# Moving DRAM sums of the output weights out of the attention stage, in a one-core hybrid encoder layer

## The chip, the core and the metric

One core of a Trainium2 chip runs the kernel. The metric is the device time of one execution in microseconds (us). The engines are named as in the profile: PE is TensorE's matmul side and PEld its weight load, DVE is VectorE, ACT is ScalarE, POOL is GpSimd, SP is SyncE, which here only issues DMAs. A name with a q behind it (SPq, ACTq) is the engine's instruction queue.

## What is computed

```python
h = rms_norm(x, norm_w)                                  # x: 512 tokens x 2048, fp32
q, k, v, g_attn, xr, g_lru = split(h @ w_in)             # 1024, 256, 256, 1024, 1024, 1024 columns
attn = softmax(rope(norm(q)) @ rope(norm(k)).T / sqrt(128)) @ v    # 8 heads over 2 kv heads
lru  = scan_forward + scan_backward of a gated recurrence on conv(xr)
mixed = concat[rms_norm(attn) * silu(g_attn), rms_norm(lru) * silu(g_lru)]
out  = x + mixed @ w_out                                 # w_out: 2048 x 2048
```

## The kernel before, in words

Every fp32 product runs as three matmuls on a high and a low part of each operand (`mm3`, lines 151 to 154). The two parts of a weight tile are made on chip from the loaded tile `wr`: ACT casts it to `wh` (line 216) and DVE subtracts, `wl = wr - wh` (line 217). SP loads the tiles (line 205) into a ring of three places, so that a load waits until DVE has finished with the tile three places before.

PE's instructions stand in the order in which the program writes them. The program interleaves a "fill", which is one of the long projections, with a chain of smaller steps: `weave` takes from the fill as many steps as the chain asks for. A fill step is six matmuls of 512 columns. Stages in order of time in the profile: two groups of the LRU input, the key and value projection, the two groups of queries (about 165 to 252 us), the attention woven into three of the four gate groups (about 270 to 432 us), the fourth gate group (to about 475 us), and the output product to the end.

The output product is done by a scheme with seven products in place of eight, on blocks of 256 tokens and of sums of the weights. The sums are made in DRAM, by DMAs alone. A plain copy puts a block of `w_out` into a DRAM buffer (`copy_to`, line 779, issued by SP), and a DMA with accumulation adds a second block to it (`add_to`, line 782, issued by POOL). The buffers are `t1`, `t2`, `t4`, `t30` and `t31`, each with eight blocks of 128 x 512 (256 KB). `t30` and `t31` are finished by `first_sums` (17 steps), which also copies the first terms into `t1` and `t2`. `last_sums` then does 32 steps: 8 adds into `t2`, 8 copies of `t2` to `t4`, 8 adds into `t1` and 8 adds into `t4`. The output product reads `t1` and `t2` first (lines 850 and 854) and `t4` later (line 875). In the profile these buffers are all called `t`; in the order of instructions further down `t_103` is t1, `t_104` is t2, `t_105` is t4, `t_106` and `t_107` are t30 and t31.

`first_sums` steps at every 8th fill step of the second LRU input group and of the key and value projection, and at every 5th fill step of the queries. `last_sums` steps once for each of the 32 softmax steps of the attention.

The attention works on one head and 128 queries at a time, 32 such units. For one unit, PE makes the scores (`weights`, line 594), DVE the negated maximum `mx` (599), ACT the exponential `p` with its sum `sm` (601), DVE the reciprocal (602), POOL the scaling of `p` (603), and DVE a transposition inside 32 x 32 blocks into `u` (604). Two units, half a head, then go through DRAM to be laid out anew: SP writes `u` to `pd` (612) and reads it back as `pt` in four DMAs (619). ACT casts `pt` to `ph`, DVE makes `pl = pt - ph` (both line 623). When both halves of a head are done, PE multiplies with the values (`values`, line 632): the first matmul reads `ph` (L152 in the profile), the second `pl` (L153), and all other PE work stands behind them. DVE also has the split of the gate weights (217), the evacuation `ev` of finished gate groups (390), the gate products (691) and the split of the next head's queries `q` (553).

The order on PE, and on SP within the attention, is the written one. ACT, DVE and POOL are ordered there by a scheduler with priorities. `tc.issue_after(i)` keeps an instruction from being put ahead of instruction `i`; it adds nothing at run time where both are on one engine. `last_scale` holds the latest scaling of `p` on POOL (603).

Of the kernel before, what the change touches and what calls it, by code (L numbers as in the profile page):

```python
# [14 lines left out]
ALU = mybir.AluOpType  # L15
# [3 lines left out]
SEQ = 512  # L19
# [36 lines left out]
C_Q, C_K, C_GA, C_XR, C_GL = 0, 1024, 1536, 2560, 3584  # L56
# [6 lines left out]
def hybrid_kernel(  # L63
# [20 lines left out]
    nc = tc.nc  # L84
# [54 lines left out]
    def pj():  # L139
        return ps.tile([P, SEQ], F32, tag="pj", name=nm("pj"))  # L140
# [4 lines left out]
    def const(shape, name, dt=F32):  # L145
        return cp.tile(list(shape), dt, tag=name, name=name)
# [4 lines left out]
    def mm3(acc, lh, ll, rh, rl, start, stop):  # L151
        nc.tensor.matmul(acc, lh, rh, start=start, stop=False)  # L152
        nc.tensor.matmul(acc, lh, rl, start=False, stop=False)  # L153
        nc.tensor.matmul(acc, ll, rh, start=False, stop=stop)  # L154
# [8 lines left out]
    nhalf = const([P, 48], "nhalf")  # L163
# [56 lines left out]
    def wload(w, r0, c0):  # L220
        with tc.high_priority(AHEAD):
            (raw,) = wraw(w, r0, c0)
            return [wsplit(raw, k) for k in range(2)]
# [32 lines left out]
    def xchunk(c):  # L256
# [6 lines left out]
        xsquare(xc, c)  # L263
        yield

    def rsqrt_mean(dst, src, n, width):

        nc.gpsimd.tensor_scalar(dst, src, 1.0 / n, EPS, op0=ALU.mult, op1=ALU.add)
        nc.gpsimd.tensor_tensor(dst, dst, nhalf[:, :width], op=ALU.pow)

    rstd = const([P, NT], "rstd")
    rbc = const([P, SEQ], "rbc")
# [26 lines left out]
    def proj_feat(c0, acc, first=None, given={}, take=None):  # L299

        acc += [pj() for _ in range(4)]
        for c in range(KT // 2):
            if c == 0 and first:

                for k, (wh, wl) in enumerate(first):
                    for j, (w, x_) in enumerate(((wh, xh), (wl, xh), (wh, xl))):
                        for e in range(4):
                            nc.tensor.matmul(
                                acc[e], w[:, e * P : (e + 1) * P], x_[k],
                                start=k == 0 and j == 0, stop=False,  # L310
                            )
                            if (j, e) in ((1, 1), (2, 3)):
                                yield c, 2 * k + j - 1
                        if (k, j) == (0, 0):
                            yield None
                continue
            if take:
                ws = take()
            else:
                ws = given[c] if c in given else wload(w_in, c * 2 * P, c0)  # L320
            for e in range(4):
                es = slice(e * P, (e + 1) * P)
                for k, (wh, wl) in enumerate(ws):
                    kk = 2 * c + k
                    mm3(acc[e], wh[:, es], wl[:, es], xh[kk], xl[kk], kk == 0, kk == KT - 1)
                yield c, e
# [16 lines left out]
    def weave(fill, chain):  # L343

        for n in chain:
            for _ in range(n):
                next(fill, None)

    def drain(fill):
        for _ in fill:  # L350
            pass
# [231 lines left out]
        split_ps(turn(rot, h), q[:, 0, :], q[:, 1, :])  # L583
        return q[:, 0, :], q[:, 1, :]

    last_scale = [None]
    pts = {}

    def weights(q, g, t, turned_, first=()):

        qh, ql = q
        tt = slice(t * P, (t + 1) * P)
        sc = mm()
        mm3(sc, qh[:, tt], ql[:, tt], kth[g], ktl[g], True, True)
        mx, sm = (at(n, 6, (1,)) for n in ("mx", "sm"))
        with ExitStack() as stack:
            for ins in first:
                stack.enter_context(tc.issue_after(ins))
            nc.vector.tensor_reduce(mx, sc, axis=AX.X, op=ALU.max, negate=True)  # L599
            p = at("p", 3, (SEQ,))  # L600
            nc.scalar.activation(p, sc, AF.Exp, bias=mx, accum_out=sm)  # L601
        nc.vector.reciprocal(sm, sm)  # L602
        last_scale[0] = nc.gpsimd.tensor_scalar(p, p, sm, 0.0, op0=ALU.mult, op1=ALU.add).ins  # L603
        nc.vector.transpose(
            turned_[:, :, :, t % 2, :].rearrange("p a s c -> p s a c"),
            p.rearrange("p (s a c) -> p s a c", a=NQ, c=B),
        )
# [39 lines left out]
            nc.scalar.activation(sq, av, AF.Square)  # L647
            nc.gpsimd.tensor_add(asum, asum, sq)

    def attention(rots, transfers):  # L650

        with tc.high_priority(AHEAD):
            qs = {0: turned(rots[0], 0)}
        yield BEGIN
        last, units = NH * NT, {}
        for i in range(last + NT + LATE):
            h, t = divmod(i, NT)
            if i < last:
                if t % 2 == 0:
                    u = at("u", 4, (NQ, NT, 2, B))  # L660
                first = pts[h - 2][2:] if h > 1 and t == 1 else ()
                weights(qs[h], h // G, t, u, first)
                next(transfers, None)
                if t == 0 and h + 1 < NH:
                    qs[h + 1] = turned(rots[(h + 1) // G], (h + 1) % G)
                if t % 2:
                    units[i] = moved(u, t // 2, pts.setdefault(h, []))
            for j in (i - 1, i - 3):
                if j in units:
                    next(units[j])  # L670
            j = i - NT - LATE
            if j >= 0 and j % NT == NT - 1:
                values(j // NT, *pts.pop(j // NT)[:2])
            yield STEPS + (last <= i < last + NT)
# [44 lines left out]
    NP = DM // (2 * P)  # L719
# [27 lines left out]
    def split(*blocks):  # L747
# [17 lines left out]
    t1, t2, t4, t30, t31 = (  # L765
        dram.tile([NP, P, SEQ + 16], F32, name=t, tag=t)[:, :, :SEQ]
        for t in ("t1", "t2", "t4", "t30", "t31")
    )
    t3 = (t30, t31)

    def block(m, k, c, n=1):

        return w_out[(2 * m + k) * P : (2 * m + k + 1) * P, c * SEQ : (c + n) * SEQ]
# [7 lines left out]
    def add_to(dst, src):  # L781
        nc.gpsimd.dma_start(dst, src, accum_op=ALU.add)  # L782

    def first_sums():

        for m in range(NP + 1):
            if m < NP:
                copy_to(*((t3[g][m], block(m, 0, 2 * g)) for g in range(2)))
            if m:
                for g in range(2):  # L790
                    add_to(t3[g][m - 1], block(m - 1, 1, 2 * g))
            yield
        for m in range(NP):
            copy_to((t1[m], block(m, 0, 0)), (t2[m], t30[m]))
            yield

    def last_sums():

        for m in range(NP):
            with tc.issue_after(last_scale[0]):  # L800
                add_to(t2[m], block(m, 0, 1))
            yield
        for m in range(NP):
            copy_to((t4[m], t2[m]))
            yield
        for m in range(NP):
            with tc.issue_after(last_scale[0]):
                add_to(t1[m], block(m, 0, 1))
            yield
        for m in range(NP):  # L810
            with tc.issue_after(last_scale[0]):
                add_to(t4[m], block(m, 1, 1))
            yield

# [218 lines left out]
    with tc.high_priority():  # L1033
# [7 lines left out]
        first = [wsplit(raw, 0, nc.vector.tensor_copy)]  # L1041
# [4 lines left out]
    for step in proj_feat(C_XR, a1, first, given):  # L1046
# [8 lines left out]
        c, e = step  # L1055
# [15 lines left out]
    s1.close()  # L1071
    lru_consts()
    fill = proj_feat(C_XR + SEQ, a2)
    wsums = first_sums()

    def with_sums(fill, n, first=0):

        for k, _ in enumerate(fill):
            if k >= first and (k - first) % n == 0:
                next(wsums, None)  # L1080
            yield

    fill = with_sums(fill, 8, 16)
# [17 lines left out]
    rots = []  # L1101
# [5 lines left out]
    def both():  # L1107
        yield from q_proj(C_Q, a4)
        yield from q_proj(C_Q + SEQ, a5)

    fill = with_sums(both(), 5)
    weave(fill, kv(kvs))
    drain(fill)
    drain(wsums)

    closed("rot", "rope", "wx")
    sums["a"] = const([P, SEQ], "asum")
# [12 lines left out]
    def take():  # L1130
        fetch()
        return fetched.pop(0)

    def gates():
        todo = iter(())
        for n, (c0, row) in enumerate(((C_GL, R_LN), (C_GL + SEQ, R_LN + 4), (C_GA, R_AN))):
            acc, wait = [], 0
            for k, _ in enumerate(proj_feat(c0, acc, take=take)):
                if n == 0 and k >= 16 and k % 4 == 0:
                    normed(hp[k // 4 - 4])  # L1140
                if wait == 0:
                    wait = next(todo, 99)
                wait -= 1
                yield
            if n < 2:
                todo = gate(evac_bc(acc), hp[2 * n : 2 * n + 2], row, None)
            else:
                late.extend(evac_bc(acc))

    for _ in range(3):  # L1150
        fetch()
    fill = gates()
    with tc.manual_schedule(engines={mybir.EngineType.SP}):
        weave(fill, attention(rots, last_sums()))
    closed("att", "qkv")
    opened("fin", "right")

# [36 lines left out]
            normed(pair)  # L1194

    acc = []
    fill = proj_feat(C_GA + SEQ, acc, take=take)
    weave(fill, later())
    drain(fill)
    closed("xw")  # L1200
# [71 lines left out]
```

## Time and profile before

| | |
|---|---|
| median of 3 runs | 646.63 us (646.61 to 646.74) |
| the profiled execution's own time | 645.42 us |
| its span, first to last instruction | 643.6 us |
| mean granted TensorE clock | 0.999 |
| DVE, ACT, POOL busy | 76%, 53%, 16% of the span |
| bytes moved by DMA | 119.24 MB, 185 GB/s on average |

The span lies inside the profiled execution's own time with 1.8 us around it, and that time is 1.2 us below the median of the unprofiled runs. A matmul of 512 columns is shown as lasting about 0.39 us, but the next one starts 0.23 us later; a pause on PE shows as a longer distance between two starts.

### The profile page before, as it was taken

Reading aid. Unit: us, or ns where it says so; the run is one execution under the profiler, and the core shown is the slowest. Engines: PE = TensorE matmul, PEld = TensorE weight load, DVE = VectorE, ACT = ScalarE, POOL = GpSimd, SP = SyncE. Lnnn points to the kernel's source line nnn. Section 1 sums busy time; section 2 is a strip of 40 time slices with the busy share of each in tenths; the row PEclk is TensorE's granted clock in tenths of the full one; section 3 lists DMA queues with packets and bytes.
Section 4 is the critical chain, followed back from the end, with each engine's and each line's share of the span. In section 5 each row is a group of like instructions: output and inputs, shape, how many; then the busy total and the mean of one; then the engine's idle time right before and its main releaser. Section 6 shows DMA issues by size and latency. Waiting matters only on the chain.

```text
span 643.6 us, 8325 instructions
## 1 busy us (share of the span) xinstructions
PE 633.3 (98%) x2835; PEld 520.7 (81%) x2835; DVE 489.3 (76%) x788; ACT 342.1 (53%) x582; POOL 100.8 (16%) x137
## 2 busy tenths in 40 slices
PE   8999999999999999999999999999999999999997
PEld 6888888888888888788787878788888888888885
DVE  5879779986698862956887788638978867787775
ACT  3534799479946623454475447326545544434441
POOL 0000200212003400343124433101000001020010
PEclk9999999999999999999999999999999999999999
DMA  9844675856567431269968999952336676797252
GB/s 296 280 141 127 143 188 156 195 146 175 129 197 247 146 99 33 97 118 284 303 208 199 253 231 223 251 155 66 109 111 207 193 264 207 276 339 254 69 197 98
DMA packets 67835, 119.24 MB, mean 185 GB/s; under 512 B 5976, under 2 KB 24528, under 8 KB 67792
## 3 DMA queue, kind: packets, MB, share of 16 engines
q1 hardware_dynamic: 59760, 100.87, 48.5%
q0 software_dynamic: 7712, 17.31, 15.0%
q10 hardware_dynamic: 320, 0.53, 0.3%
q8 instruction: 22, 0.36, 0.2%
q14 instruction: 21, 0.17, 0.1%
HBM read 106.10 MB, written 33.55 MB: 217 GB/s over the span
## 4 chain that ended last, share of the span: by engine, by line
PE 78%; issue 7%; POOL 4%; DVE 4%; DMA 4%; ACT 1%; SPq 1%; ACTq 0%; DVEq 0%; POOLq 0%
PE pj L152 16%; PE pj L153 15%; PE pj L154 15%; PE mm L906 13%; PE pj L906 10%; DMA pt<-pd 3%; PE mm L153 2%; PE mm L154 2%; POOL p L603 2%; PE mm L152 2%; POOL t L782 2%; DMA wr<-in_w_in_dram 1%; PE mm L242 1%; DVE pl L623 1%; SPq L619 1%
## 5 line engine op out<-in xcount | busy, mean ns | idle before, releaser
L152 PE MATMUL pj<-x,wh 128*128 128x512 f32 x376 | 148.2, 394 | 0.0
L154 PE MATMUL pj<-x,wl 128*128 128x512 f32 x376 | 147.0, 391 | 0.0
L153 PE MATMUL pj<-x,wh 128*128 128x512 f32 x376 | 146.9, 391 | 0.0
L216 ACT CAST wh<-wr 128x512 fp32r<-128x512 f32 x143 | 85.1, 618 | 72.1 <-PE pj L154 25.7
L217 DVE TENSOR_TENSOR wl<-wr,wh 128x512 fp32r<-128x512 f32 x144 | 100.8, 731 | 26.2 <-ACT wh L216 24.4
L758 ACT CAST wh<-wr 128x1024 fp32r<-128x1024 f32 (+1 forms) x72 | 60.6, 860 | 75.1 <-PE mm L906 37.4
L759 DVE TENSOR_TENSOR wl<-wr,wh 128x1024 fp32r<-128x1024 f32 (+1 forms) x72 | 68.6, 984 | 25.7 <-ACT wh L758 25.6
L154 PEld LDWEIGHTS pj<-x,wl 128*128 128x128 f32 x376 | 70.7, 188 | 15.0
L153 PEld LDWEIGHTS pj<-x,wh 128*128 128x128 f32 x376 | 70.7, 188 | 14.7 <-DVE x L245 0.3
L152 PEld LDWEIGHTS pj<-x,wh 128*128 128x128 f32 x376 | 70.7, 188 | 14.6
L152 PE MATMUL pj<-wh,x 128*128 128x512 f32 x192 | 75.0, 391 | 0.0
L154 PE MATMUL pj<-wh,x 128*128 128x512 f32 x192 | 74.9, 390 | 0.0
L153 PE MATMUL pj<-wl,x 128*128 128x512 f32 x192 | 74.8, 390 | 0.0
L782 POOL DMA_DIRECT2D t<-in_w_out_dram x40 | 34.3, 870 | 102.8 <-DMA t<-in_w_out_dram 102.4
L906 PE MATMUL mm<-wh,ml 128*128 128x512 f32 x128 | 49.9, 390 | 0.0
L906 PE MATMUL mm<-wl,mh 128*128 128x512 f32 x128 | 49.9, 390 | 0.0
L906 PE MATMUL mm<-wh,mh 128*128 128x512 f32 x128 | 49.9, 389 | 0.0
L601 ACT ACTIVATE p<-mm,mx 128x512 f32<-128x512 f32 x32 | 21.9, 687 | 42.2 <-DVE mx L599 42.2
L154 PEld LDWEIGHTS pj<-wh,x 128*128 128x128 f32 x192 | 36.1, 188 | 7.5
L152 PEld LDWEIGHTS pj<-wh,x 128*128 128x128 f32 x192 | 36.1, 188 | 7.4
L153 PEld LDWEIGHTS pj<-wl,x 128*128 128x128 f32 x192 | 36.1, 188 | 7.4
L603 POOL TENSOR_SCALAR p<-p,sm 128x512 f32<-128x512 f32 x32 | 23.3, 728 | 97.0 <-DVE sm L602 97.0
(204 smaller groups left out, 1056.3 us busy)
## 6 DMA issues: line engine op xcount, KB each, us to landing
wr<-in_w_in_dram SPq DMA_DIRECT2D x71, 512.0 KB, 3.9
wr<-in_w_out_dram SPq DMA_DIRECT2D x24, 512.0 KB, 5.4
t<-in_w_out_dram POOLq DMA_DIRECT2D x40, 256.0 KB, 7.0
wr<-t SPq DMA_DIRECT2D x40, 256.0 KB, 5.3
pd<-u SPq DMA_DIRECT2D x16, 512.0 KB, 7.0
pt<-pd SPq DMA_DIRECT2D x64, 128.0 KB, 7.2
t<-in_w_out_dram SPq DMA_DIRECT2D x24, 256.0 KB, 5.3
t<-t SPq DMA_DIRECT2D x16, 256.0 KB, 6.1
```

The source lines that it names most:

```text
L152: nc.tensor.matmul(acc, lh, rh, start=start, stop=False)
L153: nc.tensor.matmul(acc, lh, rl, start=False, stop=False)
L154: nc.tensor.matmul(acc, ll, rh, start=False, stop=stop)
L216: copy(hi, raw[:, k, :])
L217: nc.vector.tensor_sub(lo, raw[:, k, :], f(hi))
L242: nc.tensor.transpose(pt[:, t * P : (t + 1) * P], xc[:, t, ks], ident)
L601: nc.scalar.activation(p, sc, AF.Exp, bias=mx, accum_out=sm)
L603: last_scale[0] = nc.gpsimd.tensor_scalar(p, p, sm, 0.0, op0=ALU.mult, op1=ALU.add).ins
L758: nc.scalar.copy(hi[:, to], b)
L759: nc.vector.tensor_sub(lo[:, to], b, f(hi[:, to]))
L782: nc.gpsimd.dma_start(dst, src, accum_op=ALU.add)
L906: nc.tensor.matmul(dst[s], lh[:, ts_], rh, start=i == 0 and j == 0, stop=i == 7 and j == 2)
```

## The change

The 16 adds into `t2` and `t1` move from the attention to the end of the chain of first sums, as `more_sums`, `t1` first. The chain steps at every 3rd fill step of the queries in place of every 5th, and what is left of it at every 2nd step of the first three gate groups. The copies to `t4` and the adds into it move behind the attention, into fill steps 8 to 23 of the fourth gate group. The adds are kept behind the latest POOL instruction of either kind, the scaling of `p` or a `rsqrt_mean`, in place of the latest scaling. Nothing is added or taken out.

```diff
     def rsqrt_mean(dst, src, n, width):
 
         nc.gpsimd.tensor_scalar(dst, src, 1.0 / n, EPS, op0=ALU.mult, op1=ALU.add)
-        nc.gpsimd.tensor_tensor(dst, dst, nhalf[:, :width], op=ALU.pow)
+        last_pool[0] = nc.gpsimd.tensor_tensor(dst, dst, nhalf[:, :width], op=ALU.pow).ins
...
                 weights(qs[h], h // G, t, u, first)
-                next(transfers, None)
...
+    def more_sums():
+
+        for to, c in ((t1, 1), (t2, 1)):
+            for m in range(NP):
+                with tc.issue_after(last_pool[0]):
+                    add_to(to[m], block(m, 0, c))
+                yield
+
     def last_sums():
 
-        for m in range(NP):
-            with tc.issue_after(last_scale[0]):
-                add_to(t2[m], block(m, 0, 1))
-            yield
         for m in range(NP):
             copy_to((t4[m], t2[m]))
             yield
         for m in range(NP):
-            with tc.issue_after(last_scale[0]):
-                add_to(t1[m], block(m, 0, 1))
-            yield
-        for m in range(NP):
-            with tc.issue_after(last_scale[0]):
+            with tc.issue_after(last_pool[0]):
                 add_to(t4[m], block(m, 1, 1))
             yield
...
-    wsums = first_sums()
+    wsums = itertools.chain(first_sums(), more_sums())
...
-    fill = with_sums(both(), 5)
+    fill = with_sums(both(), 3)
     weave(fill, kv(kvs))
     drain(fill)
-    drain(wsums)
...
-    fill = gates()
+    fill = with_sums(gates(), 2)
     with tc.manual_schedule(engines={mybir.EngineType.SP}):
-        weave(fill, attention(rots, last_sums()))
+        weave(fill, attention(rots))
...
     acc = []
-    fill = proj_feat(C_GA + SEQ, acc, take=take)
+    wsums = last_sums()
+    fill = with_sums(proj_feat(C_GA + SEQ, acc, take=take), 1, 8, 8 + 2 * NP)
```

PE's order is the same before and after. On POOL, in the middle of the attention, an add stands between the scalings of `p`, before:

```order
L603 TENSOR_SCALAR p_3296<-p_3296,sm_3294 128x512
L603 TENSOR_SCALAR p_3333<-p_3333,sm_3331 128x512
L782 DMA t_103<-in_w_out_dram 128x512
L603 TENSOR_SCALAR p_3377<-p_3377,sm_3375 128x512
L782 DMA t_103<-in_w_out_dram 128x512
```

All 16 adds into `t1` and `t2` now stand earlier on POOL, around the norms of the queries: `rr` is the norm of a token block of queries, `r_l` the norm of the LRU output, and the last row is the first scaling of the attention (line numbers of the changed kernel are one or two higher there than before):

```order
L271 TENSOR_TENSOR rr_2123<-rr_2123,nhalf 128x4
L782 DMA t_103<-in_w_out_dram 128x512 x5
L270 TENSOR_SCALAR r_l<-r_l 128x4
L271 TENSOR_TENSOR r_l<-r_l,nhalf 128x4
L782 DMA t_103<-in_w_out_dram 128x512 x3
L782 DMA t_104<-in_w_out_dram 128x512 x3
L270 TENSOR_SCALAR rr_2490<-rr_2490 128x4
...
L271 TENSOR_TENSOR rr_2523<-rr_2523,nhalf 128x4
L782 DMA t_104<-in_w_out_dram 128x512 x5
L604 TENSOR_SCALAR p_2712<-p_2712,sm_2710 128x512
```

Five adds now precede `r_l`, six the norms of the second query group, five the first scaling; no add is left between two scalings.

On SP, in the fourth gate group, the copies to `t4` stand between the last weight loads (`wr` from `in_w_in_dram`) and ahead of the first loads of the output product (from `t_103`):

```order
L205 DMA wr_4390<-in_w_in_dram 128x2x512
L779 DMA t_105<-t_104 128x512 x4
L205 DMA wr_4430<-in_w_in_dram 128x2x512
L779 DMA t_105<-t_104 128x512 x4
L205 DMA wr_4471<-in_w_in_dram 128x2x512
L850 DMA wr_4624<-t_103 128x512
```

Eight copies have moved there, past all of SP's transfers of the attention.

The scheduler also moves a few instructions on DVE and ACT in the second and third head of the attention. On DVE, before, up to the second `pl` of the third head:

```order
L599 TENSOR_REDUCE mx_3293<-mm_3289 128x1
L602 RECIPROCAL sm_3294<-sm_3294 128x1
L604 STREAM_TRANSPOSE u_3237<-p_3296 128x4x4x32
L623 TENSOR_TENSOR pl_3181<-pt_3182,ph_3180 128x4x4x64
L599 TENSOR_REDUCE mx_3330<-mm_3326 128x1
L553 TENSOR_TENSOR q_3339<-mm_3340,q_3339 128x512
L602 RECIPROCAL sm_3331<-sm_3331 128x1
L217 TENSOR_TENSOR wl_3217<-wr_3214,wh_3216 128x512
L217 TENSOR_TENSOR wl_3221<-wr_3214,wh_3220 128x512
L604 STREAM_TRANSPOSE u_3325<-p_3333 128x4x4x32
L623 TENSOR_TENSOR pl_3181<-pt_3253,ph_3180 128x4x4x64
```

And now:

```order
L600 TENSOR_REDUCE mx_3294<-mm_3290 128x1
L624 TENSOR_TENSOR pl_3184<-pt_3185,ph_3183 128x4x4x64
L603 RECIPROCAL sm_3295<-sm_3295 128x1
L600 TENSOR_REDUCE mx_3330<-mm_3326 128x1
L605 STREAM_TRANSPOSE u_3239<-p_3297 128x4x4x32
L555 TENSOR_TENSOR q_3338<-mm_3339,q_3338 128x512
L603 RECIPROCAL sm_3331<-sm_3331 128x1
L605 STREAM_TRANSPOSE u_3325<-p_3333 128x4x4x32
L217 TENSOR_TENSOR wl_3219<-wr_3216,wh_3218 128x512
L217 TENSOR_TENSOR wl_3223<-wr_3216,wh_3222 128x512
L624 TENSOR_TENSOR pl_3184<-pt_3254,ph_3183 128x4x4x64
```

The first `pl` of the head now stands ahead of the reciprocal and of the transposition that follows it, and the last transposition stands ahead of the two weight splits.

More of the change, by code (lines that the diff above doesn't have):

```diff
@@ L264, in xchunk @@
         yield
+    last_pool = [None]
     def rsqrt_mean(dst, src, n, width):
         nc.gpsimd.tensor_scalar(dst, src, 1.0 / n, EPS, op0=ALU.mult, op1=ALU.add)
-        nc.gpsimd.tensor_tensor(dst, dst, nhalf[:, :width], op=ALU.pow)
+        last_pool[0] = nc.gpsimd.tensor_tensor(dst, dst, nhalf[:, :width], op=ALU.pow).ins
     rstd = const([P, NT], "rstd")
@@ L584, in turned @@
         return q[:, 0, :], q[:, 1, :]
-    last_scale = [None]
     pts = {}
@@ L602, in weights @@
         nc.vector.reciprocal(sm, sm)
-        last_scale[0] = nc.gpsimd.tensor_scalar(p, p, sm, 0.0, op0=ALU.mult, op1=ALU.add).ins
+        last_pool[0] = nc.gpsimd.tensor_scalar(p, p, sm, 0.0, op0=ALU.mult, op1=ALU.add).ins
         nc.vector.transpose(
@@ L648, in values, with attention @@
             nc.gpsimd.tensor_add(asum, asum, sq)
-    def attention(rots, transfers):
+    def attention(rots):
         with tc.high_priority(AHEAD):
@@ L1073, in hybrid_kernel, with with_sums @@
     fill = proj_feat(C_XR + SEQ, a2)
-    wsums = first_sums()
-    def with_sums(fill, n, first=0):
+    wsums = itertools.chain(first_sums(), more_sums())
+    def with_sums(fill, n, first=0, end=999):
         for k, _ in enumerate(fill):
-            if k >= first and (k - first) % n == 0:
+            if first <= k < end and (k - first) % n == 0:
                 next(wsums, None)
```

## The prediction

> **What bounds the kernel now.** I read the page first: the engines' shares, then the chain that ended last.
>
> ```profile
> PE 633.3 (98%) x2835; PEld 520.7 (81%) x2835; DVE 489.3 (76%) x788; ACT 342.1 (53%) x582; POOL 100.8 (16%) x137
> PE 78%; issue 7%; POOL 4%; DVE 4%; DMA 4%; ACT 1%; SPq 1%; ACTq 0%; DVEq 0%; POOLq 0%
> ```
>
> PE is the bound. Its order does not change, so the time changes only by pauses on PE that go or come. The next view is therefore what PE waited for between 300 and 420 us, the attention. The columns are total us, times, longest.
>
> ```profile
> PE mm L153 <- DVE pl L623: 2.7, 4, 1.0
> PE mm L152 <- ACT ph L623: 0.7, 1, 0.7
> ```
>
> These are all of its waits there: four for `pl`, one for `ph`. PE's timeline at these places gives the sizes. First columns are start and shown length, the bracket is idle time and its releaser.
>
> ```profile
> 308.35 0.50 PE L153 MATMUL mm<-pl,v 128*128 128x512 f32 x1 [0.43 <-DVE pl L623]
> ...
> 342.31 0.40 PE L152 MATMUL mm<-ph,v 128*128 128x512 f32 x1
> 343.19 0.50 PE L153 MATMUL mm<-pl,v 128*128 128x512 f32 x1 [0.48 <-DVE pl L623]
> ...
> 378.54 0.50 PE L153 MATMUL mm<-pl,v 128*128 128x512 f32 x1 [0.98 <-DVE pl L623]
> ...
> 411.69 0.39 PE L153 MATMUL pj<-x,wh 128*128 128x512 f32 x1
> 411.92 0.39 PE L154 MATMUL pj<-x,wl 128*128 128x512 f32 x1
> 412.97 0.50 PE L152 MATMUL mm<-ph,v 128*128 128x512 f32 x1 [0.66 <-ACT ph L623]
> 414.23 0.50 PE L153 MATMUL mm<-pl,v 128*128 128x512 f32 x1 [0.76 <-DVE pl L623]
> 414.57 0.39 PE L154 MATMUL mm<-ph,v 128*128 128x512 f32 x1
> ```
>
> Two starts are normally 0.23 us apart (411.69 to 411.92). What is over 0.23 is lost: 343.19 - 342.31 - 0.23 = 0.65 us at 342; (412.97 - 411.92 - 0.23) + (414.23 - 412.97 - 0.23) + (414.57 - 414.23 - 0.23) = 0.82 + 1.03 + 0.11 = 1.96 us at 412. The brackets show at least 0.43 us at 308 and 0.98 us at 378. These four places, one for every second head, are the whole stock from which a gain can come in this stage.
>
> **The change part by part.** *DMA traffic taken out of the attention.* Here the median time from issue to landing (last column, us) is compared in two stretches of the attention: 300 to 340 us, in which one add is issued, and 340 to 412 us, in which 16 are.
>
> ```profile
> pt<-pd SPq DMA_DIRECT2D x20, 128.0 KB, 3.7
> t<-in_w_out_dram POOLq DMA_DIRECT2D x1, 256.0 KB, 7.3
> t<-in_w_out_dram POOLq DMA_DIRECT2D x16, 256.0 KB, 7.9
> pt<-pd SPq DMA_DIRECT2D x32, 128.0 KB, 8.3
> ```
>
> With adds in flight a read of `pt` takes 8.3 us, without them 3.7 us, although the first stretch holds most of the copies. So I take 3.7 us for all `pt` afterwards; the bounds are 3.7 and 8.3 us. The pause at 412 hangs on this, as the chain of waits shows (start, length, what):
>
> ```profile
> 403.95 7.86 DMA pt<-pd
> 411.87 1.06 ACT ph L623
> 412.95 1.24 DVE pl L623
> ```
>
> At 3.7 us `pt` is there at 403.95 + 3.7 = 407.65. What is late next is the work queued on ACT and DVE ahead of the cast and the subtraction:
>
> ```profile
> 406.51 1.13 ACT L216 CAST wh<-wr 128x512 fp32r<-128x512 f32 x2
> 408.40 1.25 DVE L217 TENSOR_TENSOR wl<-wr,wh 128x512 fp32r<-128x512 f32 x2
> ```
>
> ACT is free at 407.64, so `ph` ends at 407.65 + 1.06 = 408.71; DVE is free at 409.65, so `pl` ends at 409.65 + 1.24 = 410.89. PE would have liked to begin at 411.92 + 0.23 = 412.15. The whole 1.96 us goes, with 1.3 us to spare.
>
> *The DVE order in the third head.* The pause at 342 does not hang on a DMA; it is the queue on DVE. Rows of DVE's timeline, and one of PE's:
>
> ```profile
> 335.00 0.17 DVE L602 RECIPROCAL sm<-sm 128x1 f32<-128x1 f32 x1 [0.91 <-ACT p L601]
> 336.00 0.71 DVE L604 STREAM_TRANSPOSE u<-p 128x512 f32<-128x512 f32 x1 [0.83 <-POOL p L603]
> 336.63 1.18 DVE L623 TENSOR_TENSOR pl<-pt,ph 128x1024 fp32r<-128x1024 f32 x1
> 337.74 0.68 DVE L599 TENSOR_REDUCE mx<-mm 128x1 f32<-128x512 f32 x1
> ...
> 341.96 1.18 DVE L623 TENSOR_TENSOR pl<-pt,ph 128x1024 fp32r<-128x1024 f32 x1
> 334.75 0.39 PE L154 MATMUL mm<-kt,q 128*128 128x512 f32 x1
> ```
>
> DVE idles 0.91 + 0.83 us ahead of the first `pl`. In the new order this `pl` comes before the reciprocal, so that it fills the idle time, and the second `mx` follows the reciprocal at once. Its scores are there (334.75 + 0.39 = 335.14, the last row, from PE), so it can start at about 335.5 in place of 337.74. From that `mx` to the second `pl` there were 341.96 - 337.74 = 4.22 us. Now another transposition is in between (336.63 - 336.00 = 0.63 us), and the last one stands ahead of the two splits, where DVE may wait 0.83 us for POOL again: at most 4.22 + 0.63 + 0.83 = 5.68 us. So `pl` begins by 341.2 and ends by 342.4, where PE wants it at 342.31 + 0.23 = 342.54. The 0.65 us go as well. This is the weakest term, with 0.2 us to spare at that end and 1.6 us at the other (4.22 us); its bounds are 0 (it stays) and 0.65.
>
> *What stays.* At 378 the order on DVE is unchanged and its last predecessor waits for PE itself:
>
> ```profile
> 376.66 0.69 DVE L390 TENSOR_TENSOR ev<-pj,rbc 128x512 f32<-128x512 f32 x1 [0.29 <-PE pj L154]
> 377.27 1.22 DVE L623 TENSOR_TENSOR pl<-pt,ph 128x1024 fp32r<-128x1024 f32 x1
> ```
>
> The evacuation `ev` can't be sooner than the gate group that it empties, and `pl` stands behind it; faster DMAs don't help. The pause at 308 is likewise behind an `ev` at an unchanged place, so I leave both.
>
> *The adds on POOL in the query stage.* POOL in the query stage has its norms at these times, with the idle time ahead of them:
>
> ```profile
> 231.33 0.19 POOL L268 TENSOR_SCALAR r_l<-r_l 128x4 f32<-128x4 f32 x1 [10.56 <-DVE r_l L704]
> ...
> 255.12 0.19 POOL L268 TENSOR_SCALAR rr<-rr 128x4 f32<-128x4 f32 x1 [22.51 <-ACT sh L523]
> ...
> 275.33 0.70 POOL L603 TENSOR_SCALAR p<-p,sm 128x512 f32<-128x512 f32 x1 [11.36 <-DVE sm L602]
> ```
>
> One issue of an add takes 0.82 us (first row below, median; the second is POOL's waits for copies, the third SP's issue of the last copy). Five adds before `r_l` take 4.1 of 10.56 us, six before the query norms 4.9 of 22.51, five before the first scaling 4.1 of 11.36. All fit in idle time, so I cost them at nothing. The cover is gone if an add has to stand and wait for its copy; then the norms behind it, and the queries' first scores on PE, are late one for one. The bound below nothing is a gain through lower traffic later, which is counted above.
>
> ```profile
> L782 POOL DMA_DIRECT2D t<-in_w_out_dram x40: 797/816/1146, 65.2 to 407.7; - x40
> POOL t L782 <- DMA t<-in_w_out_dram: 102.4, 11, 21.9
> 207.65 0.55 SPq L779 DMA_DIRECT2D t<-t  x1
> ```
>
> *SP and the DMA engines in the query stage and the fourth gate group.* The moved transfers go where DMA engines are idle: the last figure but one is their busy share (columns: stretch, length, busy us and count of PE, PEld, DVE, ACT and POOL, clock, DMA share, GB/s).
>
> ```profile
> 240.00:272.00 32.00, 31.36 (x142) 25.66 (x141) 18.92 (x33) 13.16 (x44) 6.51 (x8) 1.00 0.16 51
> ...
> 432.00:465.00 33.00, 33.00 (x151) 27.39 (x150) 28.45 (x46) 16.97 (x24) 2.62 (x3) 1.00 0.25 79
> ```
>
> In the fourth gate group the eight copies pass two weight loads on SP, at 0.55 us each for SP (the row above): `wr` waits there for DVE to free one of three places, not for SP, so these 4.4 us stand in SP's own waiting time. Cost nothing; without that cover they would cost up to 4.4 us. DVE is busy 28.45 of 33 us there, but none of its work is added to.
>
> *The sum.* 645.42 - 1.96 - 0.65 = 642.81 us against the profiled execution's own time. The median of the runs is 1.21 us above it, so 646.63 - 2.61 = 644.0 us.
>
> A rule speaks against this. The Trainium skill, "Perfetto Trace Analysis", section Identifying Performance Opportunities, says that the same gap repeating on the engine that should be saturated can mean too few buffers for the next tile. The gaps do repeat, every 35 us. By that rule all four stay, and the sum is 646.6 us. The trace agrees with the pattern and not with the cause: in the rows above, those who are waited for are a DMA, ACT and DVE, and no `pl` waits for PE to free its buffer.
>
> **The rivals.** *A: one of the two pauses stays, or a like one appears.* In the head between two pauses `pl` is ready just in time, at 358.78 + 1.21 = 359.99 for a start at 360.35:
>
> ```profile
> 358.78 1.21 DVE L623 TENSOR_TENSOR pl<-pt,ph 128x1024 fp32r<-128x1024 f32 x1
> 360.35 0.40 PE L153 MATMUL mm<-pl,v 128*128 128x512 f32 x1
> ```
>
> A queue on DVE that shifts by more than 0.36 us can make a pause there. With only 412 gone, 646.63 - 1.96 = 644.7 us; with only 342 gone, 646.0 us.
>
> *B: nothing measurable.* The pauses come from the interleaving of heads on one buffer or one queue, and a `pt` that lands sooner only lets DVE run into the next wait. For it: two of the four pauses are certainly of this kind. Against it: the 7.86 us in the chain. It gives 646.6 us.
>
> *C: slower, by POOL's queue in the query stage.* If the last of the six adds ahead of the query norms has not been issued when their first input is ready at 255.12, the norms slip, and PE waits at the first scores, where it pauses today already. For it: adds have stood 102.4 us in 11 waits for their copies, up to 21.9 us. Against it: the last of those copies was issued at 207.65 before, 32 us ahead, and its place on SP is earlier now. The price is 1 us per us of delay; to come out over 0.2% slower it has to eat the 2.61 us and 1.3 more, so an add that is issued after 255.12 + 3.9 = 259.0. A wait of 21.9 us from 240 on would end at 261.9 and give 644.0 + 6.8 = 650.8 us.
>
> **How the numbers follow.** A measurement of this kernel can tell about 0.2%, 1.3 us, from no change. Chances: the forecast 0.54 (644.0 us), A 0.18 (644.7 to 646.0, about two thirds of it over 1.3 us faster), B 0.14, C and other delays 0.14. Faster: 0.54 + 0.12, and some of the forecast's spread stays on this side, 0.68; same: 0.06 + 0.14 and less rounding, 0.18; slower 0.14. The range reaches down to both stubborn pauses also gone by what the brackets show, 644.0 - 0.43 - 0.98 = 642.6, and up over B to 646.8. What lies above it is C.
>
> **What would show it.** Right: `pt` to landing near 3.7 us over 340 to 412; no wait of ACT `ph` for a DMA over 1 us; PE's waits for `pl` twice in place of four times; POOL's norms at the same places. Wrong: a wait of POOL's `rr` or `r_l` behind an add, a new pause of PE at an odd head or in the fourth gate group, or landings that stay near 8 us, since then it was not the adds that slowed them.

## The result, and the profile after

The changed kernel takes 642.40 us (median of 6 runs, 642.28 to 642.74) beside 646.62 us before (6 runs, 645.92 to 646.91); the ratio is 0.9937, 95% interval 0.9924 to 0.995. The forecast was 644.0 us with a range of 642.6 to 646.8: the sign was right, and the gain is 4.2 us in place of 2.6. In the comparisons that follow, the runs of the kernel before have medians of 646.8 to 647.8 us on their chips, so the experiments are best compared by their ratios.

The profiled execution of the kernel after took 642.37 us itself, its span 640.6 us. Its page, the engines and the chain:

```profile
PE 632.2 (99%) x2835; PEld 520.2 (81%) x2835; DVE 484.5 (76%) x788; ACT 342.8 (54%) x582; POOL 102.7 (16%) x137
PE 89%; DVE 4%; DMA 3%; ACT 1%; SPq 1%; issue 1%; POOL 1%; DVEq 0%; ACTq 0%
```

PE had 78% of the chain before and has 89% now. What PE waits for between 300 and 420 us (total us, times, longest) is now:

```profile
PE mm L153 <- DVE pl L624: 1.5, 2, 1.0
```

The four waits for `pl` are two, and the wait for `ph` is gone. PE's timeline of after at the four places:

```profile
307.15 0.40 PE L152 MATMUL mm<-ph,v 128*128 128x512 f32 x1
308.02 0.50 PE L153 MATMUL mm<-pl,v 128*128 128x512 f32 x1 [0.47 <-DVE pl L624]
...
341.98 0.40 PE L152 MATMUL mm<-ph,v 128*128 128x512 f32 x1
342.22 0.40 PE L153 MATMUL mm<-pl,v 128*128 128x512 f32 x1
...
376.08 0.40 PE L152 MATMUL mm<-ph,v 128*128 128x512 f32 x1
377.45 0.50 PE L153 MATMUL mm<-pl,v 128*128 128x512 f32 x1 [0.98 <-DVE pl L624]
...
411.09 0.39 PE L152 MATMUL mm<-ph,v 128*128 128x512 f32 x1
411.32 0.39 PE L153 MATMUL mm<-pl,v 128*128 128x512 f32 x1
```

Read as in the prediction (start to start less 0.23 us): 0.64 us is lost at 308 and 1.14 us at 377; at 342 and 411 the starts are 0.24 and 0.23 us apart, so nothing is lost. The landings of `pt` (transfers, KB, median us), in 300 to 340 and in 340 to 412:

```profile
pt<-pd SPq DMA_DIRECT2D x20, 128.0 KB, 3.3
pt<-pd SPq DMA_DIRECT2D x36, 128.0 KB, 3.4
```

The slow half of the attention, 8.3 us before, now lands as the other half does. DVE in the third head, as ordered now:

```profile
334.32 0.15 DVE L603 RECIPROCAL sm<-sm 128x1 f32<-128x1 f32 x1
334.85 0.69 DVE L600 TENSOR_REDUCE mx<-mm 128x1 f32<-128x512 f32 x1 [0.38 <-PE mm L154]
...
339.44 1.22 DVE L624 TENSOR_TENSOR pl<-pt,ph 128x1024 fp32r<-128x1024 f32 x1
```

From the second `mx` to the second `pl` there are 4.59 us, and `pl` ends at 340.66, 1.56 us ahead of its use at 342.22. On POOL, the norms of the query stage, with the idle time ahead of them:

```profile
230.94 0.19 POOL L270 TENSOR_SCALAR r_l<-r_l 128x4 f32<-128x4 f32 x1 [1.76 <-DVE r_l L704]
...
254.73 0.19 POOL L270 TENSOR_SCALAR rr<-rr 128x4 f32<-128x4 f32 x1 [11.22 <-ACT sh L525]
...
274.98 0.71 POOL L604 TENSOR_SCALAR p<-p,sm 128x512 f32<-128x512 f32 x1 [2.19 <-DVE sm L603]
```

Each still waits for its own input, and none is behind an add: the idle times have shrunk from 10.56, 22.51 and 11.36 us, and the norms stand 0.35 to 0.4 us earlier than before. In the fourth gate group PE is busy without a gap (columns as in the prediction's windows):

```profile
425.00:500.00 75.00, 75.00 (x335) 62.09 (x334) 59.45 (x84) 36.33 (x48) 9.31 (x11) 1.00 0.63 177
```

So the mechanisms came out as forecast, and yet 1.6 us more were gained. The two profiled executions differ by 645.42 - 642.37 = 3.05 us: 2.61 are the two pauses that the prediction summed, and most of the rest is a lead that after has already at POOL's first norm (41.28 us, before 41.68), ahead of everything that was moved. The medians differ by 4.22: the profiled execution lay 1.21 us under its median before, and lies 0.03 us under it now. What the prediction missed must then be mostly in the executions of the kernel before that its one profile does not show.

### The profile page after: what moved, and what is told of

Same layout as the page of the kernel before. It is cut to its first block, busy times and chain, and to the rows that moved or that the text cites. A ratio compares the mean times of both kernels' runs of the same rounds, so it can differ in the third digit from the quotient of the medians.

```text
span 640.6 us, 8313 instructions
## 1 busy us (share of the span) xinstructions
PE 632.2 (99%) x2835; PEld 520.2 (81%) x2835; DVE 484.5 (76%) x788; ACT 342.8 (54%) x582; POOL 102.7 (16%) x137
## 4 chain that ended last, share of the span: by engine, by line
PE 89%; DVE 4%; DMA 3%; ACT 1%; SPq 1%; issue 1%; POOL 1%; DVEq 0%; ACTq 0%
PE pj L152 18%; PE pj L153 18%; PE pj L154 18%; PE mm L906 13%; PE pj L906 10%; PE mm L153 3%; PE mm L154 3%; PE mm L152 3%; DMA wr<-in_w_in_dram 3%; PE mm L242 1%; PE pj L310 1%; DVE pl L624 1%; SPq L620 1%; DVE wl L217 1%; PE mm L550 0%
## 5 line engine op out<-in xcount | busy, mean ns | idle before, releaser
L217 DVE TENSOR_TENSOR wl<-wr,wh 128x512 fp32r<-128x512 f32 x144 | 96.4, 700 | 31.6 <-ACT wh L216 29.3
```

Source lines behind the costliest of these rows:

```text
L217: nc.vector.tensor_sub(lo, raw[:, k, :], f(hi))
```

## Experiments

**Which part carries the gain.** The first kernel moves only the adds into `t1` and `t2` out of the attention, as the change does; the copies to `t4` and the adds into it, the last eight of the stage, stay there.

```
-    wsums = first_sums()
+    wsums = itertools.chain(first_sums(), more_sums())
...
     def last_sums():
-            with tc.issue_after(last_scale[0]):
-                add_to(t2[m], block(m, 0, 1))
...
-            with tc.issue_after(last_scale[0]):
-                add_to(t1[m], block(m, 0, 1))
```

> Only the 16 adds into t1 and t2 move to the query stage; copies to t4 and adds into it stay in the attention, at the same units as before. Its orders on DVE and ACT are those of before. Theory (a pause needs adds in flight at that very time; the pause at the third head is DVE's order): the t4 adds at 385 to 408 us are still there, so the pauses of 0.76 us (third head) and of about 2 us (7th head) both stay, time within 0.5 us of before. Rival (the total traffic counts): two thirds of the adds are gone, so two thirds of the gain come, about 643.8 us.

Measured: 648.34 us, ratio 1.0014 (0.9997 to 1.0031), no gain from 16 of the 24 adds. PE's waits in 300 to 420 us in this kernel, and its landings of `pt` in 340 to 412 us:

```profile
PE mm L153 <- DVE pl L624: 2.7, 4, 1.0
PE mm L152 <- ACT ph L624: 1.5, 1, 1.5
```

```profile
pt<-pd SPq DMA_DIRECT2D x33, 128.0 KB, 4.8
```

All five waits of before are there, although the median landing has fallen from 8.3 to 4.8 us. The median over 70 us was the wrong measure: what counts is the one landing ahead of the 7th head, and that takes 8.58 us here, from 404.38. The opposite kernel moves only the copies and adds of `t4`, and keeps the other 16 adds in the attention:

```
     def last_sums():
...
         for m in range(NP):
-            copy_to((t4[m], t2[m]))
             yield
...
+    def late_sums():
+        for m in range(NP):
+            copy_to((t4[m], t2[m]))
+            yield
         for m in range(NP):
             with tc.issue_after(last_scale[0]):
                 add_to(t4[m], block(m, 1, 1))
             yield
...
+    wsums = late_sums()
+    fill = with_sums(proj_feat(C_GA + SEQ, acc, take=take), 1, 8, 8 + 2 * NP)
```

> Only the copies to t4 and the adds into it move to the fourth gate group; the adds into t2 and t1 stay in the attention, at the same units as before. Its orders on DVE and ACT are those of the changed kernel. Theory: both pauses go, the 7th head's because no add is in flight there, the third head's because DVE has the new order; 2.7 us less in the trace, and by theory V up to the whole 4.2 us, 642.4 to 643.9 us. Rival (total traffic): a third of the gain, about 645.2 us.

Measured: 642.76 us, ratio 0.9924 (0.9906 to 0.9941), the whole gain. PE's waits in 300 to 420 us and the landings in 340 to 412 us:

```profile
PE mm L153 <- DVE pl L623: 1.4, 2, 1.0
```

```profile
pt<-pd SPq DMA_DIRECT2D x36, 128.0 KB, 6.2
```

The two waits are those of after, at 308 and 377, although the median landing is still 6.2 us. Its order on DVE is that of the kernel after; the landings in 300 to 340 us, 3.7 us, are those of before, so at 342 it is the order that counts and not the landing. A third kernel moves the eight adds of `t4` alone; its copies stay, and the order of every compute engine is that of before:

```
     def late_sums():
-        for m in range(NP):
-            copy_to((t4[m], t2[m]))
-            yield
         for m in range(NP):
             with tc.issue_after(last_scale[0]):
                 add_to(t4[m], block(m, 1, 1))
```

> The kernel before, with nothing changed but the time of the eight adds into t4: they go out in the fourth gate group, while the copies into t4 and the adds into t2 and t1 stay in the attention. The order of PE, DVE and ACT is that of before. Theory (the pause at 412 comes from the adds in flight at 385 to 412, the pause at 342 from the order on DVE): 412 goes, 342 stays at about 0.65 us, so about 0.65 us above the kernel with all of t4 moved (642.76), 643.4 us, ratio 0.993 to 0.995. Rival (the copies into t4 at 298 to 334 count as well, or the order on DVE carries the gain at 412 too): most of the pause at 412 stays, 645.5 us or more.

Measured: 644.63 us, ratio 0.9949 (0.9936 to 0.9963). The pause at 412 is gone and the one at 342 stays, as the theory says; PE's waits there:

```profile
PE mm L153 <- DVE pl L623: 2.1, 4, 1.0
```

The time is 1.2 us above the theory's figure. Of the 1.87 us that separate it from the kernel with all of `t4` moved, 0.66 are the pause at 342 and 0.35 a new one at 361, the place that the prediction's rival A named. The profiled execution also waits 1.43 us for `wh` at 7 us, ahead of all that differs, where that of the kernel with all of `t4` moved does not wait and those of before wait up to 0.91 us; how much of this is in the medians no trace shows. The eight adds of `t4` are thus worth the larger part, and the copies' part comes through the order on DVE.

**Traffic or queue.** Here all adds stay where they were, but each carries 16 of its 128 rows (the sums are incomplete):

```
-                add_to(t4[m], block(m, 1, 1))
+                add_to(t4[m, :R], block(m, 1, 1)[:R])
```

and likewise for `t1` and `t2`, with R = 16.

> The kernel before, with every add of the attention cut to 16 of its 128 rows (an eighth of the bytes); the sums in t1, t2 and t4 are therefore incomplete. Number and place of all instructions and the orders on DVE and ACT are those of before. Theory: pt lands in under 4.5 us throughout, the 7th head's pause goes (1.96 us), the third head's 0.76 us stays because it is DVE's order; 644.7 us in the terms of the first profile, and by theory V about 643.2 us. Rival (the adds' issue on POOL is what delays p, not their traffic): no change, 646.6 us.

Measured: 643.75 us, ratio 0.9942 (0.9923 to 0.996). POOL still issues 24 adds in the attention, yet one wait fewer for `pl` is left and none for `ph`:

```profile
PE mm L153 <- DVE pl L623: 1.8, 3, 1.0
```

The pause at 412 is gone; 342 stays at 0.62 us. So it is what the adds move that delays `pt`, not their issue on POOL. Bytes and packets shrank together here (on POOL's queue in 340 to 412 us from 4.09 to 0.53 MB and from 2235 to 512), so these two are not told apart.

**The kernel before, again.** If one profile of it does not show where the time goes, more do. V is the theory that its executions differ by the length of the pause at 412 alone.

> The kernel before, unchanged, for a second profile. The measured gain was 4.2 us and the pauses that vanished from the trace add up to 2.7 us. Theory V (the DMA pauses of before differ from run to run and the first profile caught a short one): the executions of this kernel spread over about 1.5 us or more, and this profile shows more than 1.96 us of pause at the 7th head or further pauses at other heads that wait for pt. Rival O (an offset outside the attention): the same four pauses of 0.7, 0.76, 1.26 and 1.96 us again, with a span near 643.6 us.

> The kernel before once more, for the length of its pauses in another execution. Theory (the time of an execution of before varies with the pause at 412, which hangs on a DMA): the pauses at 308, 342 and 377 within 0.1 us of 0.64, 0.66 and 1.15, the one at 412 anywhere from 1.8 to 4 us, and the span moves with it. Rival (the difference between executions lies elsewhere): 412 within 0.3 us of 1.96 whatever the span.

> As the run before it: the kernel before again, for the spread of the pause at 412. Theory: span and pause at 412 move together over the executions; rival: the span moves and the pause does not.

b2 measured 647.21 us (12 runs, 646.07 to 649.43), ratio 0.9992 (0.9979 to 1.0006), and its profiled execution 646.48; b3 and b4 took 647.16 and 646.26 us. In b2 and b4 the pause at 412 is 0.6 us longer than in the first profile, by the wait for `ph`. In b3 there is something else. The windows of b4 (the figure after POOL's count is PE's granted clock):

```profile
411.00:415.00 4.00, 2.03 (x8) 1.12 (x6) 1.20 (x1) 1.45 (x2) 0.00 (x0) 1.00 1.06 319
415.00:419.00 4.00, 3.92 (x17) 3.21 (x18) 2.00 (x4) 1.00 (x3) 0.00 (x0) 1.00 1.05 251
```

And of b3:

```profile
411.00:415.00 4.00, 2.09 (x8) 1.21 (x7) 1.80 (x2) 2.18 (x3) 0.00 (x0) 1.00 1.08 312
415.00:419.00 4.00, 4.00 (x12) 3.17 (x11) 0.87 (x3) 0.00 (x0) 0.00 (x0) 0.57 1.10 230
```

PE's busy time, 3.92 and 4.00 us, hides it; the count of matmuls, 17 and 12, and the clock, 1.00 and 0.57, show it. PE's timeline of b3:

```profile
411.65 0.39 PE L154 MATMUL pj<-x,wl 128*128 128x512 f32 x1
413.18 0.49 PE L152 MATMUL mm<-ph,v 128*128 128x512 f32 x1 [1.14 <-ACT ph L623]
414.44 0.50 PE L153 MATMUL mm<-pl,v 128*128 128x512 f32 x1 [0.77 <-DVE pl L623]
...
416.10 0.63 PE L152 MATMUL mm<-ph,v 128*128 128x512 f32 x1
416.52 0.63 PE L153 MATMUL mm<-pl,v 128*128 128x512 f32 x1
```

Behind the pause the starts are 0.42 to 0.43 us apart in place of 0.23, for some eight matmuls: 1.6 us more. The clock, which is 0.50 in the windows from 416 to 418 us, was at half for 0.43 x 4 / 0.5 = 3.4 us. This gave a new theory, W: the pause itself brings the clock down, in part of the executions.

**The same pause, without a DMA.** W was tried on the kernel after by repeating one cast on ACT in the 7th head:

```
+        for _ in range(2 if half and len(pts) and max(pts) >= 6 and his is pts.get(6) else 0):
+            nc.scalar.copy(hi, pt)
         his[2:] = [nc.scalar.copy(hi, pt).ins, nc.vector.tensor_sub(lo, pt, f(hi)).ins]
```

> The kernel after, with the cast ph of the 7th head's second half done three times in place of once (two more casts of some 1.04 us on ACT; the same result is written again). No DMA moves, and the sums stay out of the attention. It makes by ACT alone a pause at 411 of about the size that the kernel before has there: ph ends at about 412.7 in place of 407.2, pl 1.2 us later, so PE stands about 1.7 + 1.0 = 2.7 us. Theory W (a pause of that length costs more than itself in part of the executions, since the clock of PE is halved for some 3.4 us behind it, as in one profile of the kernel before: 1.6 us more): the executions spread from 645.1 to 646.9, median 645.5 to 646.5. Rival V (a pause costs itself, and the spread of the kernel before comes from the DMA alone): 645.1 us with a spread of under 0.6 us.

Measured: 647.0 us (12 runs, 645.74 to 647.54), ratio 0.9996 (0.9983 to 1.0009): one pause of 2.6 us gives back all that the change gained. PE's timeline of this kernel:

```profile
411.18 0.39 PE L154 MATMUL pj<-x,wl 128*128 128x512 f32 x1
413.00 0.51 PE L152 MATMUL mm<-ph,v 128*128 128x512 f32 x1 [1.43 <-ACT ph L626]
414.25 0.50 PE L153 MATMUL mm<-pl,v 128*128 128x512 f32 x1 [0.76 <-DVE pl L626]
```

And its windows:

```profile
411.00:415.00 4.00, 1.82 (x7) 0.93 (x6) 2.59 (x3) 1.89 (x3) 0.00 (x0) 0.96 0.23 83
415.00:419.00 4.00, 4.00 (x13) 3.16 (x12) 0.34 (x1) 0.34 (x1) 0.00 (x0) 0.61 0.85 238
```

The pause is 1.59 + 1.02 us, with the DMA engines busy for 0.23 of the stretch where before had 1.06, and the clock falls all the same. The spread is back too, 1.8 us where after has 0.5. With five casts in place of one (`range(4 ...)`):

> As the run before, with five casts in place of one: ph ends at about 414.8, and PE stands about 3.7 + 1.0 = 4.7 us. Theory W: with so long a pause the clock falls in every execution, so 642.4 + 4.7 + 1.6 = 648.7 us, the profile showing a granted clock of about 0.5 over some 3.4 us behind the pause. Rival V: 647.1 us at full clock.

Measured: 649.71 us (649.47 to 651.65), ratio 1.0047 (1.0029 to 1.0065). That is 7.3 us above after: 3.74 + 1.03 us of pause, and a clock that stays low for longer than W had it. W's 648.7 us is 1.0 us too low. The windows of its profiled execution, the longest of its runs:

```profile
415.00:419.00 4.00, 2.96 (x7) 2.17 (x8) 1.22 (x1) 0.23 (x1) 0.00 (x0) 0.60 0.34 90
419.00:425.00 6.00, 6.00 (x21) 4.71 (x20) 1.92 (x2) 1.58 (x2) 1.70 (x1) 0.70 0.68 205
```

At half speed that is 0.40 x 4 / 0.5 + 0.30 x 6 / 0.5 = 6.8 us, twice 3.4.

**How often.** Three more executions of before and one of after were profiled to count:

> The kernel before again, one of three more executions, to count in how many the clock of PE falls behind the pause at 412. Theory W: in some of the three, not in all, a granted clock of about 0.5 over some 3.4 us at 415 to 419; those executions are the longer ones, by about 1.5 us at the same pause. Rival: the clock stays at 1.00 in all three, and the spread is the pause's length alone.

> As the run before it, the second of three executions of the kernel before: theory W, clock halved in some; rival, clock at 1.00.

> As the run before it, the third of three executions of the kernel before: theory W, clock halved in some; rival, clock at 1.00.

> The kernel after again. Theory W: no pause over 1.2 us, clock at 1.00 throughout, span within 0.5 us of the 640.6 of its first profile. Rival: its executions spread as those of before do.

The seven profiled executions of before, in order of time (the pause worked out as in the prediction, its wait for `ph` and its wait for `pl`; the clock from the windows):

| execution | own time, us | pause at 412, us | clock in 415 to 419 |
|---|---|---|---|
| first profile | 645.42 | 0.82 + 1.03 | 1.00 |
| b4 | 646.26 | 1.45 + 1.03 | 1.00 |
| b6 | 646.29 | 0.84 + 1.03 | 1.00 |
| b2 | 646.48 | 1.46 + 1.03 | 1.00 |
| b3 | 647.16 | 1.30 + 1.03 | 0.57 |
| b7 | 648.18 | 1.45 + 1.03 | 0.63 |
| b5 | 648.41 | 1.18 + 1.03 | 0.67 |

The clock fell in three of seven, and these are the three longest. Length does not decide it: b2 and b4 stood longer than b3 and b5 and kept the clock. The second execution of after (a2) took 642.83 us, span 641.0, with the clock at 1.00 in these windows.

The timed runs show the falls too, by their mean granted clock over the whole execution: in the profiled executions of before it is 0.998 or 0.999 where the clock held and 0.996 where it fell. Of 69 timed runs of before in these experiments, 26 show 0.997 or less, with a median of 648.5 us and none under 647.2; the other 43 have a median of 646.8 us. With the pause made on ACT, 8 of 12 runs are at 0.996 or less (median 647.06 us, the other four 645.91), and with the longer one all seven are at 0.997 or less, four of them at 0.993 or 0.994. Of the five kernels without such a pause (after, all of `t4` moved, the adds of `t4` moved, the small adds, and the last one below) no run is under 0.998. So W holds, and V only in part: some runs of before are as long as 649.45 us at 0.998, for a reason that no trace here shows.

**The two pauses that were left.** One attempt shifts the gate groups by four steps against the heads:

```
-BEGIN, STEPS, LATE = 10, 2, 3
+BEGIN, STEPS, LATE = 14, 2, 3
```

> The kernel after, with BEGIN 14 in place of 10: four steps more of the gate groups go to PE ahead of the first scores, so that a gate group ends four steps (some 5.5 us) sooner against the heads. Theory (the pauses left at 308 and 377 are pl standing behind ev on DVE, which waits for the gate group's last products; the one at 270 is the first scores standing behind a split that is late for want of other work): on DVE the four ev now stand well ahead of the second pl, both pauses go, 0.64 + 1.15 us, and the 0.85 us at 270 with them or in part: 639.8 to 640.6 us, ratio 0.989 to 0.991. Rival (the same buffers or the same interleaving bound it, and the pauses only move to other places): 642.0 us or more.

Measured: 647.39 us, ratio 0.9993 (0.9983 to 1.0004); the rival is right. PE's waits in 300 to 420 us:

```profile
PE mm L153 <- DVE pl L624: 3.6, 3, 1.4
PE mm L152 <- ACT ph L624: 0.6, 2, 0.4
```

The pause at 270 us is gone, and the fifth head, at 377 before, loses 0.28 us. But the first head, at 308 before, now loses 1.38 us (at 313), and there are new pauses of 1.64 us at the second head (331) and 2.23 us at the sixth (401). Behind the last one the granted clock is 0.50 from 404 to 407 us, a fall as in b3. Ahead of this longest pause, DVE has the gate's own products and a wait for POOL in front of `pl`:

```profile
398.91 0.74 DVE L691 SCALAR_TENSOR_TENSOR hs<-hs,vec,ev 128x512 f32<-128x512 f32 x1
399.95 0.16 DVE L603 RECIPROCAL sm<-sm 128x1 f32<-128x1 f32 x1 [0.31 <-ACT p L602]
400.94 0.71 DVE L605 STREAM_TRANSPOSE u<-p 128x512 f32<-128x512 f32 x1 [0.82 <-POOL p L604]
401.57 1.18 DVE L624 TENSOR_TENSOR pl<-pt,ph 128x1024 fp32r<-128x1024 f32 x1
```

The other attempt takes hold of the queue on DVE itself: the four `ev` are issued behind the `pl` that PE needs next.

```
-        with tc.high_priority():
+        with ExitStack() as stack:
+            stack.enter_context(tc.high_priority())
+            for ins in behind:
+                stack.enter_context(tc.issue_after(ins))
...
-                values(j // NT, *pts.pop(j // NT)[:2])
+                parts = pts.pop(j // NT)
+                done_pl[:] = parts[3:]
+                values(j // NT, *parts[:2])
...
-                todo = gate(evac_bc(acc), hp[2 * n : 2 * n + 2], row, None)
+                todo = gate(evac_bc(acc, done_pl[:1]), hp[2 * n : 2 * n + 2], row, None)
...
```

> The kernel after, with the four ev of each gate group held on DVE until the pl that PE needs next has been issued; PE, ACT and the DMAs keep their order. Theory (the pauses left at 308 and 377 are pl standing behind ev on DVE): both go, 0.64 and 1.15 us, 642.4 - 1.8 = 640.6 us, ratio about 0.990 to 0.991. Rival (the prediction's sentence that the pauses of this kind are bound by the interleaving and stay; or the four ev, now later, make a like pause where the next head's pl or the gate's products wait): 641.8 us or more.

Measured: 640.85 us (640.72 to 641.1, 4 runs), ratio 0.9904 (0.9882 to 0.9926), the fastest of all. At 377 the profile of after had an `ev` with a wait for PE ahead of `pl`:

```profile
375.57 0.69 DVE L392 TENSOR_TENSOR ev<-pj,rbc 128x512 f32<-128x512 f32 x1 [0.48 <-PE pj L154]
```

DVE at the same place in this kernel, and PE's use of this `pl`:

```profile
374.20 1.21 DVE L627 TENSOR_TENSOR pl<-pt,ph 128x1024 fp32r<-128x1024 f32 x1
375.33 1.27 DVE L395 TENSOR_TENSOR ev<-pj,rbc 128x512 f32<-128x512 f32 x2
...
376.10 0.40 PE L153 MATMUL mm<-pl,v 128*128 128x512 f32 x1
```

The `pl` ends at 375.41, ahead of its use at 376.10, and PE waits for nothing between 300 and 420 us in this kernel.

## Why the prediction was right and wrong

- **The pause at 412 goes: right, too small.** That it hangs on `pt`, and `pt` on the adds in flight, is shown by the kernels that move or shrink the adds. What failed is the size, in the step "The sum", twice. First, it took 1.96 us for this pause from one profiled execution, the shortest of seven with the shortest pause. The seven lose 1.96 to 2.60 us there, 1.21 + 1.03 + 0.11 = 2.35 us on average, and three of them 1.6 us of half clock behind it. Second, it carried this execution's 1.21 us distance to the median over as if it stayed: after the change it is 0.03 us. That is 1.18 of the 1.6 us by which the gain exceeds the forecast; the rest is about the lead at 41 us. There the seven executions of before stand at 41.3 to 42.0 and the two of after at 41.3 and 41.7, so that part is luck and not the change.
- **What made up the distance is known in part.** Between the mean of the seven executions, 646.89 us, and that of the two of after, 642.60, there are 4.29 us: 2.35 for the pause, 0.7 for the falls of the clock, 0.65 for 342, 0.16 for two pauses at 395 in b4 and b5 (0.44 and 0.66 us), and some 0.4 not assigned. But the falls hardly count in the 4.22 us between the medians of the result: the six runs of before behind 646.62 us reach 646.91 at most, and no execution of before with a fall is under 647.1. The four executions at full clock lose 2.28 us at 412 on average; with the 0.65 us that is 2.9 of the 4.22 us. The other 1.3 are not assigned, since no profiled execution at full clock is as long as that median.
- **The pause at 342 goes by DVE's order: right,** 0.65 us, with 1.56 us to spare where the prediction allowed 0.2 to 1.6. It stays in every kernel with the old order, also where `pt` lands in 4.3 us (the small adds, 340 to 412 us).
- **308 and 377 stay: right** for this change, 0.64 and 1.14 us. The remark that "faster DMAs don't help" holds, but they are no property of the schedule: another place of the `ev` in DVE's queue removed both.
- **The adds in the query stage and the transfers in the fourth gate group at nothing: right.** Rival C did not occur, nor did rival A in the kernel after.
- **Rival B and the rule of too few buffers: wrong here.** The gaps that repeat went without one buffer more: one by traffic, one by order on DVE by the change, and two by order in the last experiment.
- **The range** allowed a lower end only by 308 and 377 going as well, and had no term for executions of before that are longer than the profiled one. For those two it used the brackets, 0.43 and 0.98 us; by the measure of its other terms, start to start, the profile before shows 0.59 and 1.15 us, and the lower end would have been 642.3. It would have held the result only by luck, since both pauses stayed. A profiled time 1.21 us under a median of three runs that agree to 0.13 us was the sign: whatever that distance consists of can go with the pause, or stay.

## What to carry to other kernels

Size a pause from several executions, and ask whether the profiled one is typical of the timed ones; a distance between them belongs in the range. The mean granted clock of each timed run shows which of them lost time to the clock. When taking a DMA burst out of a stage, look at what is in flight at the one transfer that PE waits for, not at the stage's median. Where an engine's queue holds a critical operation behind one that waits for PE, ordering these two on the queue can be worth more than moving work.

## What was not expected of the hardware

A pause of PE of 2.2 to 2.6 us, broken by one matmul, brought the granted clock to half for some 3.4 us in three of seven profiled executions of the kernel before and in that with the pause made on ACT, and so cost up to 1.6 us more than itself. The Trainium skill, "TensorE: Matmul & The Clock Gate", section "What's actually happening", has a clock that falls to half after an idle window of about 3.4 us, and windows that run freely, not from the kernel's start. The runs agree with the half and with the 3.4 us (6.8 us behind the longest pause); and whether the clock fell did not follow the pause's length (1.46 + 1.03 us without, 1.18 + 1.03 us with), as windows that run freely would have it. They differ in that a shorter and interrupted idle time was enough.
